# First weights on a second issuing queue, the norm vector inside the first x^T transfer, the last stores on two queues, and a gate product moved ahead

## The chip, the cores and the metric

The kernel runs on one core of a Trainium2 chip. The metric is the device time of one execution in microseconds (us). The kernel before takes 1500.37 us, the median of three runs (1499.43 to 1500.54).

## The reference

One layer of a streaming encoder on 256 tokens of width 2048, all in float32. Shapes are given as (rows x columns).

```python
u = rmsnorm(x, norm_mix)                                   # 256 x 2048
z = u @ w_in                                               # 2048 x 15360
p, q, k, v, g_ret, g_pool, g_rt = split(z)                 # 1024, 1024, 1024, 2048, 2048, 2048, 2048
y_pool = pool_branch(p, w_group, scale) @ w_pool_proj      # 1024 x 2048: trailing means, linear map
y_ret  = retention_branch(q, k, v, g_ret) @ w_ret_proj     # 2048 x 2048: 8 heads, GroupNorm, silu gate
merged = sigmoid(g_pool) * y_pool + sigmoid(g_rt) * y_ret
h = x + merged @ w_out                                     # 2048 x 2048
ug = rmsnorm(h, norm_ffn) @ w_up                           # 2048 x 11264: gate half, up half
gate = causal_conv3(ug[:, :5632], conv_w) + conv_b
h = h + (silu(gate) * ug[:, 5632:]) @ w_down               # 5632 x 2048
out = h * rsqrt(mean(h * h) + 1e-6) * norm_final
```

## The kernel before, in words

Every large product is done to nearly float32 accuracy with float32r matmuls: each operand is cut into a high part (`hi`, written by ScalarE, line 82) and the rest (`lo`, by VectorE, line 83), and `mm3` (lines 89 to 92) adds three matmuls, hi by hi, hi by lo and lo by hi. Weights come in blocks of 128 partitions x 2048 floats (1 MB) on SyncE's queue (line 97), three buffers deep. A block is four k-tiles of 128 x 512 (in `w_up` it is 16 of 128 x 128). Its two halves of 128 x 1024 are split one after the other into three pairs of `hi` and `lo` buffers.

`product` (lines 213 to 227) makes 512 output columns for both blocks of 128 tokens (`tb` 0 and 1): per k-tile six matmuls of 512 columns. Its two sums sit in one of two PSUM pairs (`acc_pair`, two buffers in turn), so that a product needs the pair of the product before last. After each four k-tiles `tick` runs one small step from the list `side` (transposes, retention, pooling).

The stages follow one another: the first product with `w_in` (lines 155 to 173, operands arriving in small pieces), the rest of `w_in` with rotary embedding, retention and pooling, the sigmoid gates, then lines 459 to 486, the merge, then `w_out`, `w_up` with the convolution, and `w_down`. A tile framework orders the instructions of each engine and places the semaphores; a DMA takes one of eight completion semaphores in turn, and waits until the DMA that had it before has landed.

The places that the change touches:

- The head, lines 133 to 173. VectorE clears `warm`, ten bf16 matmuls on it occupy TensorE, and SyncE issues the norm vector (`nmix`, 128 x 16, line 143), then by turns a piece of x^T (line 160, 256 columns per k-tile) and a piece of weights (line 162, 512 columns per k-tile): first one k-tile each, again one, and then two at a time. Line 86 (ScalarE) multiplies x^T by `nmix` and rounds it to the high part, line 87 (VectorE) makes the rest, and lines 82 and 83 do the weights.
- The merge. For each of four column blocks `nb`, a product with `w_pool_proj` (8 k-tiles, sums `psp`) is followed by one with `w_ret_proj` (16 k-tiles, `psr`). Behind both, VectorE multiplies `psp` by its sigmoid (line 471) and `psr` by its own (line 472) and adds (line 473), for `tb` 0 and then 1.
- The tail, lines 588 to 667. `residual` adds the last sums to `h` in two halves (line 594), squares them with a running sum (line 597, ScalarE) and multiplies by the final norm vector (line 600). `finish` makes 1/sqrt of the mean square (lines 605 to 613) and scales and stores four pieces of 128 x 512 (lines 619 to 622), by VectorE and ScalarE in turn, all stored by SyncE. `finish` for `tb` 0 runs beside the matmuls of `tb` 1; for `tb` 1 nothing runs beside it.

Of the kernel before, what the change touches and what calls it, by code (L numbers as in the profile page):

```python
# [16 lines left out]
P = 128  # L17
D = 2048
# [25 lines left out]
def tile_block(ctx: ExitStack, tc: tile.TileContext, ins, out):  # L44
# [85 lines left out]
            side.popleft()()  # L130


    warm = const.tile([P, NB], BF16, tag="warm", name="warm")
    dve.memset(warm, 0.0)
    warm_a = small.tile([P, 1], F32, tag="warm_a", name="warm_a", bufs=1)
# [3 lines left out]
        pe.matmul(warm_ps, warm[:, :P], warm, start=True, stop=True)  # L139


    nmix = const.tile([P, KT], F32, tag="nmix", name="nmix")
    sp.dma_start(nmix, ins["nmix"])
    uh = [unit(F32R) for _ in range(2)]
    ul = [unit(F32R) for _ in range(2)]

    def kview(pair, kt):
        return pair[kt // 8][:, (kt % 8) * T : (kt % 8 + 1) * T]

    NB_P, NB_Q, NB_K, NB_V, NB_GR, NB_SP, NB_SR = 0, 2, 4, 6, 10, 14, 18  # L150
    first = {}
    xt = [unit() for _ in range(2)]
    raws = {}
    done = 0
    for n in (1, 1) + (2,) * 7:
        g, at = divmod(done, 4)
        if at == 0:
            raws[g] = wraw.tile([P, 2048], F32, tag="raw", name=nm("raw"))
        x2 = xt[done // 8][:, (done % 8) * T : (done % 8 + n) * T]
        sp.dma_start(x2, ins["xt"][:, done * T : (done + n) * T])  # L160
        w2 = raws[g][:, at * NB : (at + n) * NB]
        sp.dma_start(w2, ins["w_in"][NB_Q * 4 + g][:, at * NB : (at + n) * NB])
        for j in range(n):
            k = done + j
            split_scaled(kview(uh, k), kview(ul, k), x2[:, j * T : (j + 1) * T], nmix[:, k : k + 1])
        if at % 2 == 0:
            hi = wsplit.tile([P, 1024], F32R, tag="hi", name=nm("hi"))
            lo = wsplit.tile([P, 1024], F32R, tag="lo", name=nm("lo"))
            first[g, at // 2] = (hi, lo)
        for j in range(n):  # L170
            o = slice((at + j) % 2 * NB, ((at + j) % 2 + 1) * NB)
            split(hi[:, o], lo[:, o], w2[:, j * NB : (j + 1) * NB])
        done += n


    trig = const.tile([P, 2 * TB * 64], F32, tag="trig", name="trig")
# [282 lines left out]
    for nb in range(4):  # L459
        psp = product(  # L460
            ins["w_pool_proj"],
            nb * 2,
            8,
            lambda k: mix_h[:, k * T : (k + 1) * T],
            lambda k: mix_l[:, k * T : (k + 1) * T],
        )
        psr = product(ins["w_ret_proj"], nb * 4, KT, lambda k: kview(ret_h, k), lambda k: kview(ret_l, k))
        for tb in range(TB):
            a, b = t2k(), t2k()
            s = slice(tb * 1024 + (nb % 2) * NB, tb * 1024 + (nb % 2 + 1) * NB)  # L470
            dve.tensor_tensor(a, psp[tb], sgp[nb // 2][:, s], ALU.mult)  # L471
            dve.tensor_tensor(b, psr[tb], sgr[nb // 2][:, s], ALU.mult)  # L472
            dve.tensor_tensor(a, a, b, ALU.add)

            def turn(a=a, nb=nb, tb=tb):
                pt = aux_tile()
                for c in range(4):
                    pe.transpose(pt[:, c * P : (c + 1) * P], a[:, c * P : (c + 1) * P], ident)  # L478
                n0 = (nb % 2) * 4
                dst = [  # L480
                    x[nb // 2].rearrange("p (k t) -> p k t", t=T)[:, n0 : n0 + 4, tb * P : (tb + 1) * P]
                    for x in (mg_h, mg_l)
                ]
                split(dst[0], dst[1], pt.rearrange("p (c t) -> p c t", t=P))

            side.append(turn)
# [101 lines left out]
    def residual(tb, nb, ps):  # L588

        n = NB // 2 if nb == 3 else NB  # L590
        g = t2k() if nb == 3 else h[tb][:, nb * NB : (nb + 1) * NB]
        for c in range(0, NB, n):
            s = slice(nb * NB + c, nb * NB + c + n)
            dve.tensor_tensor(h[tb][:, s], ps[:, c : c + n], h[tb][:, s], ALU.add)
            junk = t2k()
            i = nb + c // n
            act.activation(junk[:, :n], h[tb][:, s], AF.Square, accum_out=ssq3[:, tb, i : i + 1])
        for c in range(0, NB, n):
            s = slice(nb * NB + c, nb * NB + c + n)
            dve.tensor_tensor(g[:, c : c + n], h[tb][:, s], gf[:, s], ALU.mult)  # L600
        return g

    def finish(tb, last):
        a, v, y, q = (small.tile([P, 1], F32, tag=f"fin{i}", name=nm("fin")) for i in range(4))
        dve.tensor_scalar(a, ssq3[:, tb, 3:4], 1.0 / D, part[:, tb : tb + 1], ALU.mult, ALU.add)
        act.activation(y, ssq3[:, tb, 4:5], AF.Sqrt, scale=1.0 / D, bias=a)
        dve.tensor_scalar(v, ssq3[:, tb, 4:5], 1.0 / D, a, ALU.mult, ALU.add)

        r = small.tile([P, 1], F32, tag="fin_r", name=nm("r"))
        dve.reciprocal(y, y)  # L610
        dve.tensor_scalar(q, y, y, v, ALU.mult, ALU.mult)
        dve.tensor_scalar(q, q, -0.5, 1.5, ALU.mult, ALU.add)
        dve.tensor_tensor(r, y, q, ALU.mult)
        for nb in range(4):
            s = slice(nb * NB, (nb + 1) * NB)
            g = last if nb == 3 else h[tb][:, s]
            o = t2k()
            if nb % 2 == 0:
                dve.tensor_scalar(o, g, r, None, ALU.mult)
            else:  # L620
                act.activation(o, g, AF.Copy, scale=r)
            sp.dma_start(out[tb * P : (tb + 1) * P, s], o)

    for nb in range(3):
        ps = product(ins["w_down"], nb * 11, NFF, lambda k: kview(ah, k), lambda k: kview(al, k))
# [12 lines left out]
    for g in range(NFF // 4):  # L638
# [11 lines left out]
        for hf, (wh, wl) in enumerate(halves):  # L650
            for j in range(2):
# [9 lines left out]
                    mm(1)  # L661
                else:
                    held.append(mm)
    finish(0, residual(0, 3, ps[0]))
    for mm in held:
        mm(1)
    finish(1, residual(1, 3, ps[1]))

# [11 lines left out]
def _arrays(np, x, norm_mix, w_in, w_pool_group, pool_scale, w_pool_proj, ret_gn_gain,  # L682
            w_ret_proj, w_out, norm_ffn, w_up, conv_w, conv_b, w_down, norm_final):
    f = np.float32
    a = {}
    x = np.asarray(x)[0]
    a["xt"] = np.ascontiguousarray(x.T.reshape(KT, P, T).transpose(1, 0, 2)).reshape(P, KT * T)
    a["x"] = x.reshape(TB, P, D)
    a["w_in"] = _blocks(np.asarray(w_in)[0], np)
    a["w_pool_proj"] = _blocks(np.asarray(w_pool_proj)[0], np)  # L690
    a["w_ret_proj"] = _blocks(np.asarray(w_ret_proj)[0], np)
    a["w_out"] = _blocks(np.asarray(w_out)[0], np)
    a["w_down"] = _blocks(np.asarray(w_down)[0], np)
    up = np.asarray(w_up)[0].reshape(KT, P, 2, NFF, P).transpose(3, 2, 1, 0, 4)
    a["w_up"] = np.ascontiguousarray(up).reshape(2 * NFF, P, KT * P)
    g = np.asarray(w_pool_group)[0].reshape(4, 2, P, 256).transpose(2, 0, 1, 3)
    a["w_pool_group"] = np.ascontiguousarray(g).reshape(P, 2048)
    cw = np.asarray(conv_w)[0].reshape(3, NFF, P).transpose(2, 0, 1).reshape(P, 3 * NFF)
    a["vecs"] = np.concatenate(
        [  # L700
            _columns(np.asarray(norm_ffn)[0]),
            _columns(np.asarray(ret_gn_gain)[0]),
            _columns(np.asarray(pool_scale)[0]),
            cw,
            _columns(np.asarray(conv_b)[0]),
        ],
        axis=1,
    )
    a["nmix"] = np.ascontiguousarray(_columns(np.asarray(norm_mix)[0]))
    a["norm_final"] = np.asarray(norm_final).reshape(1, D)  # L710

    t = np.arange(T)
    inv = 10000.0 ** (-np.arange(64) / 64.0)
    ang = t[:, None].astype(f) * inv.astype(f)[None, :]
    ang = ang.astype(np.float64)
    trig = np.stack([np.cos(ang), np.sin(ang)], axis=1).astype(f)
    a["trig"] = np.ascontiguousarray(trig.reshape(TB, P, 128).transpose(1, 0, 2)).reshape(P, 2 * TB * 64)
    log_g = np.log(1.0 - 2.0 ** (-5.0 - np.arange(HEADS)))
    j, i = t[:, None], t[None, :]
    gap = np.where(j // CHUNK <= i // CHUNK, np.abs(i - j), np.inf)  # L720
# [30 lines left out]
```

## Time and profile before

| | |
|---|---|
| time, median of 3 | 1500.37 us |
| profiled execution | 1500.19 us, of which the span in the trace is 1498.4 us |
| granted TensorE clock | 0.998 of full speed |
| TensorE busy | 1480.2 us, 99% of the span |
| VectorE / ScalarE busy | 911.1 us (61%) / 698.2 us (47%) |
| DMA | 287.01 MB, mean 192 GB/s; 336 GB/s in the first fortieth of the span |

TensorE is busy at 9 tenths or more in each of the forty slices but the last. Busy time alone therefore says little about where time can be saved: the waits and the chain of work show it.

### The profile page before, as it was taken

The page shows a single profiled execution, that of the slowest core. Times are in us where ns is not written, and L with a number is a line of the kernel's source. Part 1 is how long each engine was busy: PE and PEld are TensorE (multiplying, and loading weights), DVE is VectorE, ACT ScalarE, POOL GpSimd, SP SyncE. Part 2 cuts the span into 40 slices and gives each one's busy share as a digit, 9 for nine tenths or more (in the row PEclk, how much of TensorE's full clock was granted, in tenths as well). Part 3 has the DMA queues.
Part 4 walks back from the last instruction along what each step waited for, and adds up shares of the span by engine and source line. Part 5 has one row for each costly group of instructions (what it writes and reads, how often), then busy time and mean ns, then how long its engine had stood idle before and what let it go on. Part 6 is the DMA issues. An engine that isn't in the chain of part 4 may idle for free.

```text
span 1498.4 us, 18277 instructions
## 1 busy us (share of the span) xinstructions
PE 1480.2 (99%) x7286; PEld 1243.5 (83%) x7286; DVE 911.1 (61%) x1229; ACT 698.2 (47%) x899; POOL 0.2 (0%) x4
## 2 busy tenths in 40 slices
PE   9999999999999999999999999999999999999997
PEld 6888888888888877778888888888888888888886
DVE  5765865675444455555577777777766766445454
ACT  6545444455444433334455444444454444344343
POOL 0000000000000000000000000000000000000000
PEclk9999999999999999999999999999999999999999
DMA  9654555464555555565545555555555555555553
GB/s 336 208 204 161 189 192 195 165 212 178 171 194 197 197 180 185 197 211 182 191 174 193 176 194 185 182 196 178 187 194 176 193 187 211 195 194 196 197 196 113
DMA packets 42710, 287.01 MB, mean 192 GB/s; under 512 B 4993, under 2 KB 5633, under 8 KB 9089
## 3 DMA queue, kind: packets, MB, share of 16 engines
q1 hardware_dynamic: 42624, 285.84, 54.9%
q8 instruction: 57, 0.93, 0.2%
q14 instruction: 29, 0.23, 0.0%
HBM read 283.73 MB, written 2.10 MB: 191 GB/s over the span
## 4 chain that ended last, share of the span: by engine, by line
PE 98%; DVE 1%; DMA 1%; SPq 0%; issue 0%; ACT 0%; ACTq 0%
PE acc L90 21%; PE acc L92 20%; PE acc L91 20%; PE acc L556 20%; PE acc L557 10%; PE acc L560 1%; PE aux L91 1%; PE aux L92 1%; PE aux L90 1%; PE acc L559 1%; DMA raw<-in_w_in 1%; PE aux L248 0%; PE aux L478 0%; PE aux L341 0%; DVE lo L83 0%; DVE t L472 0%
## 5 line engine op out<-in xcount | busy, mean ns | idle before, releaser
L83 DVE TENSOR_TENSOR lo<-raw,hi 128x1024 fp32r<-128x1024 f32 (+1 forms) x526 | 634.6, 1208 | 460.3 <-ACT hi L82 460.2
L82 ACT ACTIVATE hi<-raw 128x1024 fp32r<-128x1024 f32 (+1 forms) x526 | 549.3, 1046 | 588.6 <-PE acc L92 438.8
L90 PE MATMUL acc<-hi,u 128*128 128x512 f32 x1336 | 524.1, 392 | 5.9 <-DVE t L471 5.9
L92 PE MATMUL acc<-hi,u 128*128 128x512 f32 x1336 | 520.6, 390 | 0.0
L91 PE MATMUL acc<-lo,u 128*128 128x512 f32 x1336 | 520.0, 389 | 0.0
L556 PE MATMUL acc<-u,hi 128*128 128x512 f32 x1320 | 470.2, 399 | 0.0
L557 PE MATMUL acc<-u,lo 128*128 128x256 f32 x1320 | 370.8, 281 | 0.0
L90 PEld LDWEIGHTS acc<-hi,u 128*128 128x128 f32 x1336 | 250.9, 188 | 57.8 <-ACT hi L82 7.5
L556 PEld LDWEIGHTS acc<-u,hi 128*128 128x128 f32 x1320 | 248.0, 188 | 56.9
L92 PEld LDWEIGHTS acc<-hi,u 128*128 128x128 f32 x1336 | 250.7, 188 | 53.3
L91 PEld LDWEIGHTS acc<-lo,u 128*128 128x128 f32 x1336 | 251.1, 188 | 50.3
L557 PEld LDWEIGHTS acc<-u,lo 128*128 128x128 f32 x1320 | 249.3, 189 | 4.2
L565 ACT ACTIVATE t<-acc 128x256 f32<-128x256 f32 x88 | 29.1, 382 | 70.5 <-PE acc L560 70.5
L568 DVE TENSOR_TENSOR t<-acc,t 128x256 f32<-128x256 f32 x88 | 33.3, 420 | 45.5 <-ACT t L565 45.5
L82 ACT ACTIVATE u<-t 128x256 fp32r<-128x256 f32 x44 | 18.3, 417 | 51.6 <-DVE t L578 51.6
L560 PE MATMUL acc<-u,hi 128*128 128x512 f32 x88 | 35.2, 400 | 0.0
L570 DVE TENSOR_TENSOR t<-t,rb 128x512 f32<-128x512 f32 x44 | 30.5, 693 | 1.5
L83 DVE TENSOR_TENSOR u<-t,u 128x256 fp32r<-128x256 f32 x44 | 18.6, 424 | 19.3 <-ACT u L82 19.3
L86 ACT ACTIVATE u<-aux,vecs 128x256 fp32r<-128x256 f32 x40 | 18.7, 469 | 23.6 <-DVE u L87 22.7
L559 PE MATMUL acc<-u,lo 128*128 128x256 f32 x88 | 24.9, 283 | 0.0
L87 DVE SCALAR_TENSOR_TENSOR u<-aux,vecs,u 128x256 fp32r<-128x256 f32 x40 | 19.1, 481 | 8.7 <-ACT u L86 8.7
L271 ACT ACTIVATE u<-acc,y 128x512 f32<-128x512 f32 x24 | 15.2, 686 | 17.0 <-PE acc L92 17.0
(132 smaller groups left out, 538.9 us busy)
## 6 DMA issues: line engine op xcount, KB each, us to landing
raw<-in_w_up SPq DMA_DIRECT2D x88, 1024.0 KB, 4.9
raw<-in_w_in SPq DMA_DIRECT2D x84, 1024.0 KB, 4.9
raw<-in_w_down SPq DMA_DIRECT2D x44, 1024.0 KB, 4.9
raw<-in_w_ret_proj SPq DMA_DIRECT2D x16, 1024.0 KB, 4.9
raw<-in_w_out SPq DMA_DIRECT2D x16, 1024.0 KB, 4.9
raw<-in_w_pool_proj SPq DMA_DIRECT2D x8, 1024.0 KB, 5.0
u<-in_x SPq DMA_DIRECT2D x4, 1024.0 KB, 7.7
raw<-in_w_in SPq DMA_DIRECT2D x7, 512.0 KB, 8.5
```

The lines of the kernel that those rows point to most:

```text
L82: act.activation(hi, src, AF.Copy)
L83: dve.tensor_tensor(lo, src, plain(hi), ALU.subtract)
L90: pe.matmul(o, ah, bh, start=start, stop=False)
L91: pe.matmul(o, ah, bl, start=False, stop=False)
L92: pe.matmul(o, al, bh, start=False, stop=stop)
L556: pe.matmul(o[half], wh[:, s], both, start=kt == 0, stop=False)
L557: pe.matmul(o[half][:, :T], wl[:, s], both[:, :T], start=False, stop=False)
L559: pe.matmul(o[half][:, :T], wl[:, s], both[:, :T], start=False, stop=False)
L560: pe.matmul(o[half], wh[:, s], both, start=False, stop=True)
L565: act.activation(small_part[:, half * T : (half + 1) * T], o[half][:, T:], AF.Copy)
L568: dve.tensor_tensor(gu[:, h2], o[half][:, :T], small_part[:, h2], ALU.add)
L570: dve.tensor_tensor(gv, gv, rb.unsqueeze(1).broadcast_to([P, 2, T]), ALU.mult)
```

## The change

Four edits, which are independent in what they compute; the output is the same function of the inputs.

1. The head. The norm vector is put in front of x^T in device memory, so that one row of that input is 16 + 4096 floats, and the first transfer brings `nmix` and the first piece of x^T as one tile `front` of 128 x 272. The first three pairs of transfers are issued ahead of the clearing of `warm`, and the two weight pieces of one k-tile each go out on ScalarE's queue.
2. The merge. The two multiplications of `psp` by its sigmoid stand between the two products.
3. The tail's scalar chain. The first addend `a` is computed between the two halves of the multiplication by the final norm vector.
4. The stores. ScalarE scales the first quarter and stores it by its own queue; VectorE scales the other three, and SyncE stores them.

```diff
+    front = const.tile([P, KT + T], F32, tag="front", name="front")
+    nmix = front[:, :KT]
+    pieces = ((0, 1), (1, 1)) + tuple((k, 2) for k in range(2, KT, 2))
...
+    def load_x(k, n):
+        if k == 0:
+            return sp.dma_start(front, ins["xt"][:, : KT + T])
+        return sp.dma_start(x_piece(k, n), ins["xt"][:, KT + k * T : KT + (k + n) * T])
+
+    def load_w(k, n, eng):
+        return eng.dma_start(w_piece(k, n), ins["w_in"][NB_Q * 4 + k // 4][:, k % 4 * NB : (k % 4 + n) * NB])
+
+    for k, n in pieces[:3]:
+        tc.keep_in_program_order(load_x(k, n))
+        tc.keep_in_program_order(load_w(k, n, act if n == 1 else sp))
...
-    nmix = const.tile([P, KT], F32, tag="nmix", name="nmix")
-    sp.dma_start(nmix, ins["nmix"])
...
-        sp.dma_start(x2, ins["xt"][:, done * T : (done + n) * T])
...
-        sp.dma_start(w2, ins["w_in"][NB_Q * 4 + g][:, at * NB : (at + n) * NB])
+        if k0 > 2:
...
+            load_x(k0, n)
+            load_w(k0, n, sp)
...
+        cols = [slice(tb * 1024 + (nb % 2) * NB, tb * 1024 + (nb % 2 + 1) * NB) for tb in range(TB)]
+        gated = [t2k() for _ in range(TB)]
+        for tb in range(TB):
+            dve.tensor_tensor(gated[tb], psp[tb], sgp[nb // 2][:, cols[tb]], ALU.mult)
         psr = product(ins["w_ret_proj"], nb * 4, KT, lambda k: kview(ret_h, k), lambda k: kview(ret_l, k))
         for tb in range(TB):
-            a, b = t2k(), t2k()
-            s = slice(tb * 1024 + (nb % 2) * NB, tb * 1024 + (nb % 2 + 1) * NB)
-            dve.tensor_tensor(a, psp[tb], sgp[nb // 2][:, s], ALU.mult)
-            dve.tensor_tensor(b, psr[tb], sgr[nb // 2][:, s], ALU.mult)
+            a, b = gated[tb], t2k()
+            dve.tensor_tensor(b, psr[tb], sgr[nb // 2][:, cols[tb]], ALU.mult)
             dve.tensor_tensor(a, a, b, ALU.add)
...
+            if c:
+
+                a = small.tile([P, 1], F32, tag="fin0", name=nm("fin"))
+                dve.tensor_scalar(a, ssq3[:, tb, 3:4], 1.0 / D, part[:, tb : tb + 1], ALU.mult, ALU.add)
             dve.tensor_tensor(g[:, c : c + n], h[tb][:, s], gf[:, s], ALU.mult)
...
-        dve.tensor_scalar(a, ssq3[:, tb, 3:4], 1.0 / D, part[:, tb : tb + 1], ALU.mult, ALU.add)
...
-            if nb % 2 == 0:
+            if nb:
                 dve.tensor_scalar(o, g, r, None, ALU.mult)
             else:
                 act.activation(o, g, AF.Copy, scale=r)
-            sp.dma_start(out[tb * P : (tb + 1) * P, s], o)
+            (sp if nb else act).dma_start(out[tb * P : (tb + 1) * P, s], o)
...
-    a["xt"] = np.ascontiguousarray(x.T.reshape(KT, P, T).transpose(1, 0, 2)).reshape(P, KT * T)
+    xt = np.ascontiguousarray(x.T.reshape(KT, P, T).transpose(1, 0, 2)).reshape(P, KT * T)
+    a["xt"] = np.concatenate([_columns(np.asarray(norm_mix)[0]), xt], axis=1)
```

On VectorE, at the end of the first column block of the merge, this stands before. `acc_3949` holds the sums of the `w_pool_proj` product of this block, `acc_4018` those of its `w_ret_proj` product, and `acc_4165` those of the next block's `w_pool_proj` product, which takes the pair of `acc_3949`; lines 471, 472 and 473 are the two gates and the addition.

```order
L472 TENSOR_TENSOR t_4156<-acc_4018,u_2699 128x512
L471 TENSOR_TENSOR t_4160<-acc_3949,u_2697 128x512
L473 TENSOR_TENSOR t_4155<-t_4155,t_4156 128x512
L472 TENSOR_TENSOR t_4161<-acc_4018,u_2699 128x512
L83 TENSOR_TENSOR lo_4210<-raw_4207,hi_4209 128x1024
L473 TENSOR_TENSOR t_4160<-t_4160,t_4161 128x512
L83 TENSOR_TENSOR lo_4214<-raw_4207,hi_4213 128x1024
L83 TENSOR_TENSOR lo_4252<-raw_4249,hi_4251 128x1024
L83 TENSOR_TENSOR u_3947<-aux_4200,u_3945 128x4x128
L83 TENSOR_TENSOR lo_4256<-raw_4249,hi_4255 128x1024
L471 TENSOR_TENSOR t_4385<-acc_4165,u_2697 128x512
```

On VectorE, the same place after the change. `acc_4021` is now the `w_ret_proj` pair, `acc_4164` the next block's `w_pool_proj` pair; lines 489, 493 and 494 are the gates and the addition.

```order
L493 TENSOR_TENSOR t_4158<-acc_4021,u_2698 128x512
L493 TENSOR_TENSOR t_4161<-acc_4021,u_2698 128x512
L494 TENSOR_TENSOR t_4017<-t_4017,t_4158 128x512
L494 TENSOR_TENSOR t_4018<-t_4018,t_4161 128x512
L83 TENSOR_TENSOR lo_4209<-raw_4206,hi_4208 128x1024
L83 TENSOR_TENSOR lo_4213<-raw_4206,hi_4212 128x1024
L83 TENSOR_TENSOR lo_4255<-raw_4252,hi_4254 128x1024
L83 TENSOR_TENSOR u_3946<-aux_4199,u_3944 128x4x128
L83 TENSOR_TENSOR lo_4259<-raw_4252,hi_4258 128x1024
L489 TENSOR_TENSOR t_4247<-acc_4164,u_2696 128x512
L489 TENSOR_TENSOR t_4248<-acc_4164,u_2696 128x512
```

The gate of `tb` 1's `w_pool_proj` sums has left the group behind the `w_ret_proj` product and stands with that of `tb` 0 behind the `w_pool_proj` product; in front of the third `lo` half of the next block (`lo_4210`, now `lo_4209`) there are four instructions as before.

On SyncE's queue, at the program's start, this stands before; `u` is the buffer of x^T, `raw` that of the weights.

```order
L143 DMA nmix<-in_nmix 128x16
L160 DMA u_100<-in_xt 128x256
L162 DMA raw_102<-in_w_in 128x512
L160 DMA u_100<-in_xt 128x256
L162 DMA raw_102<-in_w_in 128x512
L160 DMA u_100<-in_xt 128x512
L162 DMA raw_102<-in_w_in 128x1024
L160 DMA u_100<-in_xt 128x512
L162 DMA raw_129<-in_w_in 128x1024
```

On SyncE's queue after the change, the same transfers up to the weights of k-tiles 4 and 5 (`raw_128`):

```order
L148 DMA front<-in_xt 128x272
L149 DMA u_80<-in_xt 128x256
L149 DMA u_80<-in_xt 128x512
L152 DMA raw_82<-in_w_in 128x1024
L149 DMA u_80<-in_xt 128x512
L152 DMA raw_128<-in_w_in 128x1024
```

Three issues have left SyncE's queue: `nmix` is gone, and the first two weight pieces stand on ScalarE's queue, ahead of its table load. The eight instructions in front of the weights of k-tiles 4 and 5 have become five.

On VectorE, at the end of the program (`tb` 1), before and then after the change; `ssq` holds the sums of squares, `u_9963` and `u_9962` the final norm vector.

```order
L594 TENSOR_TENSOR u_4861<-acc_11121,u_4861 128x256 x2
L600 TENSOR_TENSOR t_11527<-u_4861,u_9963 128x256 x2
L605 TENSOR_SCALAR fin_11536<-ssq_9965,part 128x1
L607 TENSOR_SCALAR fin_11537<-ssq_9965,fin_11536 128x1
L610 RECIPROCAL fin_11538<-fin_11538 128x1
```

```order
L616 TENSOR_TENSOR u_4860<-acc_11120,u_4860 128x256 x2
L626 TENSOR_TENSOR t_11526<-u_4860,u_9962 128x256
L625 TENSOR_SCALAR fin_11534<-ssq_9964,part 128x1
L626 TENSOR_TENSOR t_11526<-u_4860,u_9962 128x256
L632 TENSOR_SCALAR fin_11537<-ssq_9964,fin_11534 128x1
L635 RECIPROCAL fin_11538<-fin_11538 128x1
```

The addend of line 605 (now 625) has moved in front of the second half of the multiplication.

## Rows read from the trace of the kernel before

**Rows 1.** The page's chain of work that ended last, by engine.

```profile
PE 98%; DVE 1%; DMA 1%; SPq 0%; issue 0%; ACT 0%; ACTq 0%
```

**Rows 2.** Waits of TensorE: line, waited for, us in total, times, longest.

```profile
PE acc L90 <- DVE t L471: 5.9, 4, 1.5
```

**Rows 3.** Timeline, first merge boundary: start, us, engine, line, operation [idle before].

```profile
552.03 0.39 PE L92 MATMUL acc<-hi,u 128*128 128x512 f32 x1
...
552.45 0.69 DVE L472 TENSOR_TENSOR t<-acc,u 128x512 f32<-128x512 f32 x1 [0.40 <-PE acc L92]
553.06 0.68 DVE L471 TENSOR_TENSOR t<-acc,u 128x512 f32<-128x512 f32 x1
...
553.89 0.47 PE L90 MATMUL acc<-hi,u 128*128 128x512 f32 x1 [1.47 <-DVE t L471]
...
554.26 0.68 DVE L472 TENSOR_TENSOR t<-acc,u 128x512 f32<-128x512 f32 x1
...
554.86 1.22 DVE L83 TENSOR_TENSOR lo<-raw,hi 128x1024 fp32r<-128x1024 f32 x1
```

**Rows 4.** The chain in order of time: merge boundaries, products of w_out.

```profile
552.19 0.24 PE acc L92
...
587.56 0.24 PE acc L92
...
688.45 0.44 PE aux L511 x4
...
711.18 0.44 PE aux L511 x4
```

**Rows 5.** Timeline of SyncE's queue at the start, duration of each issue.

```profile
0.73 0.39 SPq L143 DMA_DIRECT2D nmix<-in_nmix  x1
1.17 0.42 SPq L160 DMA_DIRECT2D u<-in_xt  x1
...
4.48 0.56 SPq L162 DMA_DIRECT2D raw<-in_w_in  x1
```

**Rows 6.** Timeline of the start, the other engines.

```profile
3.55 0.51 ACT L86 ACTIVATE u<-u,nmix 128x256 fp32r<-128x256 f32 x1 [1.33 <-DMA u<-in_xt]
...
12.96 1.15 ACT L82 ACTIVATE hi<-raw 128x512 fp32r<-128x512 f32 x2 [0.41 <-DMA raw<-in_w_in]
...
13.62 1.29 DVE L83 TENSOR_TENSOR lo<-raw,hi 128x512 fp32r<-128x512 f32 x2 [0.56 <-ACT hi L82]
...
14.37 0.50 PE L91 MATMUL aux<-lo,u 128*128 128x512 f32 x1 [0.22 <-DVE lo L83]
```

**Rows 7.** Stretches of the start: busy PE, PEld, DVE, ACT, POOL; clock, DMA share, GB/s.

```profile
2.00:3.00 1.00, 1.00 (x4) 0.44 (x3) 0.00 (x0) 0.21 (x2) 0.00 (x0) 1.00 0.55 168
3.00:4.00 1.00, 1.00 (x4) 0.32 (x3) 0.00 (x0) 0.45 (x1) 0.00 (x0) 1.00 0.81 178
4.00:5.00 1.00, 1.00 (x4) 0.25 (x2) 0.48 (x1) 0.06 (x1) 0.00 (x0) 1.00 0.83 189
...
14.00:16.00 2.00, 1.78 (x8) 1.39 (x8) 2.00 (x5) 1.91 (x5) 0.00 (x0) 1.00 1.03 408
```

**Rows 8.** Timeline of the tail after the last matmul.

```profile
1490.42 0.75 DVE L600 TENSOR_TENSOR t<-u,u 128x256 f32<-128x256 f32 x2
1490.53 0.19 ACT L597 ACTIVATION_READ_ACCUMULATOR t<-u 128x1 f32 x1
...
1490.93 0.18 ACT L597 ACTIVATION_READ_ACCUMULATOR t<-u 128x1 f32 x1
1491.09 0.21 DVE L605 TENSOR_SCALAR fin<-ssq,part 128x1 f32<-128x1 f32 x1
1491.39 0.29 ACT L606 ACTIVATE fin<-ssq,fin 128x1 f32<-128x1 f32 x1 [0.28 <-DVE fin L605]
...
1492.61 0.88 DVE L619 TENSOR_SCALAR t<-u,r 128x512 f32<-128x512 f32 x2
```

**Rows 9.** A stretch of the last stores, columns as in Rows 7.

```profile
1494.00:1495.00 1.00, 0.00 (x0) 0.00 (x0) 0.00 (x0) 0.00 (x0) 0.00 (x0) 0.50 1.02 385
```

More of the change, by code (lines that the diff above doesn't have):

```diff
@@ L130, in flush, with x_piece, w_piece @@
             side.popleft()()
+    front = const.tile([P, KT + T], F32, tag="front", name="front")
+    nmix = front[:, :KT]
+    xt = [unit() for _ in range(2)]
+    NB_P, NB_Q, NB_K, NB_V, NB_GR, NB_SP, NB_SR = 0, 2, 4, 6, 10, 14, 18
+    raws = {0: wraw.tile([P, 2048], F32, tag="raw", name=nm("raw"))}
+    pieces = ((0, 1), (1, 1)) + tuple((k, 2) for k in range(2, KT, 2))
+    def x_piece(k, n):
+        return front[:, KT:] if k == 0 else xt[k // 8][:, (k % 8) * T : (k % 8 + n) * T]
+    def w_piece(k, n):
+        return raws[k // 4][:, k % 4 * NB : (k % 4 + n) * NB]
+    def load_x(k, n):
[7 more added lines that the diff above has]
+        tc.keep_in_program_order(load_w(k, n, act if n == 1 else sp))
     warm = const.tile([P, NB], BF16, tag="warm", name="warm")
@@ L148, in kview @@
         return pair[kt // 8][:, (kt % 8) * T : (kt % 8 + 1) * T]
-    NB_P, NB_Q, NB_K, NB_V, NB_GR, NB_SP, NB_SR = 0, 2, 4, 6, 10, 14, 18
     first = {}
[L152 to L159, printed above, removed]
-        sp.dma_start(x2, ins["xt"][:, done * T : (done + n) * T])
-        w2 = raws[g][:, at * NB : (at + n) * NB]
-        sp.dma_start(w2, ins["w_in"][NB_Q * 4 + g][:, at * NB : (at + n) * NB])
+    for k0, n in pieces:
+        g, at = divmod(k0, 4)
+        if k0 > 2:
+            if at == 0:
+                raws[g] = wraw.tile([P, 2048], F32, tag="raw", name=nm("raw"))
+            load_x(k0, n)
+            load_w(k0, n, sp)
+        x2, w2 = x_piece(k0, n), w_piece(k0, n)
         for j in range(n):
-            k = done + j
+            k = k0 + j
             split_scaled(kview(uh, k), kview(ul, k), x2[:, j * T : (j + 1) * T], nmix[:, k : k + 1])
@@ L172, in tile_block @@
             split(hi[:, o], lo[:, o], w2[:, j * NB : (j + 1) * NB])
-        done += n
     trig = const.tile([P, 2 * TB * 64], F32, tag="trig", name="trig")
@@ L591, in residual @@
         g = t2k() if nb == 3 else h[tb][:, nb * NB : (nb + 1) * NB]
+        a = None
         for c in range(0, NB, n):
@@ L599, in residual, with finish @@
             s = slice(nb * NB + c, nb * NB + c + n)
+            if c:
+                a = small.tile([P, 1], F32, tag="fin0", name=nm("fin"))
+                dve.tensor_scalar(a, ssq3[:, tb, 3:4], 1.0 / D, part[:, tb : tb + 1], ALU.mult, ALU.add)
             dve.tensor_tensor(g[:, c : c + n], h[tb][:, s], gf[:, s], ALU.mult)
-        return g
-    def finish(tb, last):
-        a, v, y, q = (small.tile([P, 1], F32, tag=f"fin{i}", name=nm("fin")) for i in range(4))
-        dve.tensor_scalar(a, ssq3[:, tb, 3:4], 1.0 / D, part[:, tb : tb + 1], ALU.mult, ALU.add)
+        return g, a
+    def finish(tb, last, a):
+        v, y, q = (small.tile([P, 1], F32, tag=f"fin{i}", name=nm("fin")) for i in range(1, 4))
         act.activation(y, ssq3[:, tb, 4:5], AF.Sqrt, scale=1.0 / D, bias=a)
@@ L663, in tile_block @@
                     held.append(mm)
-    finish(0, residual(0, 3, ps[0]))
+    finish(0, *residual(0, 3, ps[0]))
     for mm in held:
         mm(1)
-    finish(1, residual(1, 3, ps[1]))
+    finish(1, *residual(1, 3, ps[1]))
 def _blocks(w, np):
@@ L708, in _arrays @@
     )
-    a["nmix"] = np.ascontiguousarray(_columns(np.asarray(norm_mix)[0]))
     a["norm_final"] = np.asarray(norm_final).reshape(1, D)
```

## The prediction

> **What bounds the kernel now.** I read the chain of waits first: 98% of the time that decides the end lies on TensorE [rows 1]. A change can then gain only where TensorE stands still, and this one touches the three places where it does: the start, the four ends of a merge block, and the tail behind the last matmul. The view of waits gives the middle one: four waits of TensorE for line 471, 5.9 us in all, 1.5 the longest [rows 2]. The timeline shows what one is [rows 3]. The last matmul of a block begins at 552.03. Its sums come free for VectorE at 552.45, which does line 472 for `tb` 0 first and line 471 for `tb` 1 behind it, to about 553.7. Only that line frees the PSUM pair that the next block's first matmul writes, and it starts at 553.89. The pair's sums had been complete since the end of the `w_pool_proj` product, sixteen k-tiles earlier. VectorE was told to read them late.
>
> At the start the chain is a transfer: the weights of k-tiles 4 and 5 are issued at 4.48 [rows 5] and reach ScalarE at 12.96. Its split, and VectorE's, let the matmul at 14.37 go [rows 6]. That is the last wait of the first product.
>
> **The merge (part 2).** What a boundary costs is best taken from the chain. From one block's end to the next is 587.56 - 552.19 = 35.37 us [rows 4]. A product with `w_out` has the sixteen k-tiles and two sets of four transposes without such a wait: 711.18 - 688.45 = 22.73 us [rows 4]. Less two transposes at 0.44, that is 21.85 us for 96 matmuls, 0.228 each. The merge block has 48 matmuls more, so 22.73 + 10.92 = 33.65 without a wait, and 35.37 - 33.65 = 1.72 us are lost. The wait alone is 1.47 [rows 3]; the rest is restarting. The ends are 4 x 1.47 = 5.9 and 4 x 1.72 = 6.9. I take 6.9, since it counts whole periods.
>
> What is late next? VectorE still has four instructions behind a block's end, and behind them the third `lo` half of the next block, at 554.86 for 1.22 us, so ready at 556.1 [rows 3]. TensorE, no longer held, needs that half after 24 matmuls and four transposes: 552.03 + 0.23 + 5.47 + 0.44 = 558.2. That leaves 2.1 us. In the middle of the block line 489 now runs twice, 0.69 each, ahead of the third `lo` half of `w_ret_proj`: about 0.4 + 1.4 + 1.2 = 3.0 us behind the product's end, where the two halves already split last 5.5. The pair of `psr` is free 1.8 us into the next block, which needs it 11 us in. No new wait of TensorE follows, and the work added is none: the same twelve multiplications and additions, in another order.
>
> **The head (part 1).** Three issues leave SyncE's queue ahead of the deciding transfer. The first x^T piece takes the place of `nmix`, 1.17 - 0.73 = 0.44 us earlier, and the deciding issue is five issues of about 0.45 behind 0.73, at 3.0 instead of 4.48: 1.5 us earlier [rows 5]. But a transfer that is issued earlier lands earlier only where the DMA engines had room. Between 2 and 5 us they were busy 0.55, 0.81 and 0.83 of the time [rows 7]: 0.45 + 0.19 + 0.17 = 0.81 us of room, a part of it because the second and third transfers were not yet issued. The start itself moves by 0.44. So 0.44 is had from the earlier start alone, up to 1.25 with all the room filled. I take 0.8, between the two. ScalarE's two issues, 2 x 0.47 = 0.94 at SyncE's pace, lie in the 1.33 us in which it stood idle ahead of its first x^T piece [rows 6]. When that piece comes 0.44 earlier, 0.05 us of cover is lost, at a place where TensorE is not yet waited for. The bounds are wide, since the trace has no transfer on ScalarE's queue and no row of x^T that begins 64 bytes into a line. At best the DMA moves at the 408 GB/s of 14 to 16 us from the start [rows 7], which is a rival below. At worst the x^T of six k-tiles, 786 KB, goes at the 178 GB/s of 3 to 4 us instead of 408 [rows 7]: 4.4 us instead of 1.9, a loss of 2.5 less the 0.44, so 2.0.
>
> A rule of the Trainium skill speaks against this part (DMA: Bandwidth & Descriptors, "How a descriptor splits into AXI transactions"): a descriptor that doesn't start on a multiple of 256 bytes needs one read more, so a 2 KB row nine instead of eight. By that rule, an estimate from the page, x^T would take an eighth longer, 0.2 us on the way to the deciding transfer; the head would give 0.6 and the sum come to 7.7. No row of this trace shows it.
>
> **The tail (parts 3 and 4).** The addend (line 605) starts at 1491.09 behind both halves of line 600, although its sum of squares was read out at 1490.53 + 0.19 = 1490.72. The square root (line 606) waits for it until 1491.39 [rows 8]. Between the halves the addend can start at about 1490.42 + 0.38 = 1490.80 and is done at 1491.01. The root then waits for its other input, read out at 1490.93 + 0.18 = 1491.11, and starts near 1491.15: 0.24 earlier. VectorE's second half and the instruction behind it end some 0.1 later than the root, if nothing overlaps; so 0.12 to 0.24, and I take 0.2. For the stores, VectorE's first output, ready about 0.45 us behind 1492.61, goes to SyncE at once in both kernels, and from 1494 on the DMA engines are full, at 1.02 of their time and 385 GB/s [rows 9]. Four stores of 256 KB then take 2.7 us however they are issued. Cover: the engines are the bound, not the issuing queue; worth 0, with the tail's 0.2 from the earlier start alone. For `tb` 0 the same edits lie beside the matmuls of `tb` 1 and cost nothing.
>
> **Sum.** 6.9 + 0.8 + 0.2 = 7.9 us. The profiled execution took 1500.19, 1.8 more than its span: 1500.19 - 7.9 = 1492.3. The median of the runs is 0.18 above that execution. I forecast 1492.3.
>
> **Rivals.**
> - *The start runs at full rate.* With two queues filled at once the DMA moves 408 GB/s from 2 us on. The 2.36 MB up to k-tile 5 need 5.8 us, and TensorE is bound by its own 24 matmuls: it begins near 5 us, when the warming matmuls end [rows 7], and reaches k-tile 4 at about 10.6 instead of 14.4, 3.8 earlier: 1500.19 - 6.9 - 3.8 - 0.2 = 1489.3. For it: the low GB/s of 2 to 5 us. Against it: the engines were already busy 0.8 there. Chance 0.12.
> - *The head loses*, by the worst bound: 1500.19 - 6.9 + 2.0 - 0.2 = 1495.1. Chance 0.08.
> - *A wait takes the place of the one removed.* If VectorE comes 2.1 us later than counted at a boundary, TensorE stands before the third `lo` half and the merge gives nothing: 1500.19 - 0.8 - 0.2 = 1499.2. Against it: the order in front of that half is four instructions as before. Chance 0.06, half of that with part of the gain left.
> - *Slower: x^T comes too slowly to feed the first product.* Rows that start 64 bytes late are read f times slower. Two k-tiles need 262 KB of x^T (0.64 us at 408 GB/s) and 524 KB of weights (1.29), while TensorE takes 24 x 0.228 = 5.5 us for four, 2.7 for two. The first six k-tiles lose 1.9 x (f - 1), and each of the five later pairs 1.29 + 0.64 f - 2.7. From about f = 3.4 this eats the 7.9; at f = 4 it is 5.7 + 5 x 1.15 = 11.5, and the time 1503.8. Against it: between 2 and 5 us, at its slowest, the DMA was 408 / 168 = 2.4 times slower than later [rows 7]. Chance 0.03.
>
> **How the numbers follow.** The forecast has 0.71, the rivals 0.12, 0.08, 0.06 and 0.03. The range, 1490.0 to 1495.2, holds the forecast's own spread (head 0 to 1.5, merge 5.9 to 6.9: 1491.5 to 1494.3), a third of the first rival and the second: about 0.82. A measurement of this kernel can tell a change of about 0.2%, 3.0 us, from none. Faster than 1497.4: 0.71 + 0.12 + 0.08 + 0.03 of the third, 0.94. Within 3 us: 0.03. Slower: 0.03.
>
> **What would show it.** In the profile after, TensorE has no wait for a merge gate, and blocks follow one another every 33.6 to 33.7 us. The last wait of the first product ends near 13.6 instead of 14.37, the root starts 0.2 us sooner behind the last matmul, and the stores keep the DMA engines full as before. A wait of TensorE for a `lo` half 6 us into a merge block, or blocks over 34 us, would break the first term; a last head wait later than 14.4 the second.

## The result: 8.8 us faster, and the profile after

The changed kernel takes 1491.24 us, the median of four runs (1490.98 to 1491.49). The kernel before took 1500.07 beside it (1499.43 to 1500.54). The ratio is 0.9941, with a 95% interval of 0.9924 to 0.9959. The profiled execution takes 1491.38 us against 1500.19, so 8.81 less, where the sum had 7.9.

Three marks in the trace split this: the first transposes behind the first product, the last transposes inside the `w_out` product, and the last matmul. The lines are from the timeline of TensorE (start, us, engine, line, operation), of the kernel before:

```profile
74.10 0.60 PE L248 MATMUL aux<-ident,t 128*128 128x128 f32 x4
...
754.29 0.60 PE L511 MATMUL aux<-ident,u 128*128 128x128 f32 x4
...
1489.33 0.39 PE L92 MATMUL acc<-u,u 128*128 128x512 f32 x1
```

The same marks after:

```profile
72.39 0.60 PE L267 MATMUL aux<-ident,t 128*128 128x128 f32 x4
...
745.55 0.60 PE L532 MATMUL aux<-ident,u 128*128 128x128 f32 x4
...
1480.68 0.39 PE L92 MATMUL acc<-u,u 128*128 128x512 f32 x1
```

The first mark comes 1.71 us earlier, which is the head. From the first to the second it was 680.19 and is 673.16: 7.03 less, the merge. From the second to the third it is 735.04 and 735.13, so 0.09 more, in a stretch that the change doesn't touch. The span ends 9.09 behind the start of the last matmul before, and 8.91 after: the tail, 0.18. Together 8.83.

**The merge.** These are all the waits of TensorE in the kernel after (what, total, times, longest). The group of four for 5.9 us [rows 2] is gone, and nothing has come in its place:

```profile
PE aux L165 <- DVE warm L160: 1.2, 1, 1.2
PE aux L90 <- ACT hi L82: 0.4, 1, 0.4
PE aux L91 <- DVE lo L83: 0.2, 1, 0.2
PE aux L556 <- DVE dg L555: 0.2, 1, 0.2
```

The first boundary in the timelines of TensorE and VectorE, against [rows 3]:

```profile
550.32 0.39 PE L92 MATMUL acc<-hi,u 128*128 128x512 f32 x1
550.54 0.39 PE L90 MATMUL acc<-hi,u 128*128 128x512 f32 x1
...
550.74 1.29 DVE L493 TENSOR_TENSOR t<-acc,u 128x512 f32<-128x512 f32 x2 [0.40 <-PE acc L92]
551.95 1.28 DVE L494 TENSOR_TENSOR t<-t,t 128x512 f32<-128x512 f32 x2
553.15 1.22 DVE L83 TENSOR_TENSOR lo<-raw,hi 128x1024 fp32r<-128x1024 f32 x1
...
556.66 0.40 PE L91 MATMUL acc<-lo,u 128*128 128x512 f32 x1
```

The next block's first matmul starts 0.22 behind the last one; before the change it started 1.86 behind. VectorE still does its four instructions, now beside TensorE. The third `lo` half is ready at 553.15 + 1.22 = 554.37, and the matmul at 556.66 is its first reader: 2.3 us of slack. The chain shows the period, here by the first transposes of the first and of the fourth block's result, against [rows 4]:

```profile
556.15 0.44 PE aux L499 x4
...
656.99 0.44 PE aux L499 x4
```

Three periods lie between: (656.99 - 556.15) / 3 = 33.61 us each, instead of 35.37.

**The head.** Timeline of the start after, against [rows 5, 6]:

```profile
0.73 0.91 ACTq L152 DMA_DIRECT2D raw<-in_w_in  x2
0.73 0.38 SPq L148 DMA_DIRECT2D front<-in_xt  x1
...
3.21 0.74 SPq L152 DMA_DIRECT2D raw<-in_w_in  x1
...
4.95 0.51 ACT L86 ACTIVATE u<-front 128x256 fp32r<-128x256 f32 x1 [1.79 <-DMA front<-in_xt]
...
8.52 1.16 ACT L82 ACTIVATE hi<-raw 128x512 fp32r<-128x512 f32 x2 [0.37 <-DMA raw<-in_w_in]
...
9.93 0.50 PE L91 MATMUL aux<-lo,u 128*128 128x512 f32 x1 [0.22 <-DVE lo L83]
...
10.47 1.15 ACT L82 ACTIVATE hi<-raw 128x512 fp32r<-128x512 f32 x2
```

The weights of k-tiles 4 and 5, issued at 3.21 instead of 4.48, are split from 10.47 on, 2.49 us earlier than the 12.96 of [rows 6], and are waited for no longer: the row at 10.47 has no idle time in front of it. TensorE's last wait of the first product ends at 9.93, on the weights of k-tiles 2 and 3. Twelve matmuls, 2.73 us, lie between that matmul and the one of k-tile 4 where it used to wait until 14.37, so its end answers to 14.37 - 2.73 = 11.64, and 11.64 - 9.93 = 1.71 is the gain. On the other side, x^T's first piece reaches ScalarE at 4.95, later than the 3.55 of [rows 6].

The stretches of the start after (columns as in [rows 7]):

```profile
2.00:3.00 1.00, 1.00 (x4) 0.44 (x3) 0.00 (x0) 0.99 (x2) 0.00 (x0) 1.00 0.88 195
3.00:4.00 1.00, 1.00 (x4) 0.31 (x3) 0.00 (x0) 0.16 (x1) 0.00 (x0) 1.00 0.92 175
4.00:5.00 1.00, 1.00 (x4) 0.30 (x2) 0.00 (x0) 0.05 (x1) 0.00 (x0) 1.00 0.97 305
5.00:8.00 3.00, 2.60 (x9) 1.27 (x7) 2.30 (x5) 2.86 (x6) 0.00 (x0) 1.00 1.00 378
8.00:11.00 3.00, 2.78 (x12) 1.95 (x12) 2.58 (x6) 2.63 (x6) 0.00 (x0) 1.00 0.99 387
```

The last two of them before:

```profile
5.00:8.00 3.00, 1.76 (x7) 1.16 (x7) 1.69 (x3) 1.84 (x4) 0.00 (x0) 1.00 0.95 335
8.00:11.00 3.00, 2.54 (x10) 1.52 (x9) 1.91 (x4) 1.84 (x4) 0.00 (x0) 1.00 0.94 302
```

Between 2 and 5 us the DMA moved 140 KB more than before, 675 instead of 535; between 5 and 11 us 384 KB more, 3 x (43 + 85).

**The tail.** Timeline behind the last matmul after, against [rows 8]:

```profile
1482.50 0.29 ACT L631 ACTIVATE fin<-ssq,fin 128x1 f32<-128x1 f32 x1
...
1483.72 0.72 ACT L646 ACTIVATE t<-u,r 128x512 f32<-128x512 f32 x1 [0.92 <-DVE r L638]
...
1484.48 0.35 ACTq L647 DMA_DIRECT2D out<-t  x1
```

The root starts 1.82 us behind the last matmul's start, and started 2.06 behind it before (1491.39 - 1489.33): 0.24 earlier. The stores' stretch, against [rows 9]:

```profile
1485.00:1488.00 3.00, 0.00 (x0) 0.00 (x0) 0.00 (x1) 0.00 (x0) 0.00 (x0) 0.50 0.97 349
```

The DMA engines are nearly full again, and from the start of the output's first scaling to the last landing it is 4.98 us in both kernels. The second queue gave nothing there.

### The profile page after: what moved, and what is told of

Same layout as the page of the kernel before. It is cut to its first block, busy times and chain, and to the rows that moved or that the text cites. A ratio compares the mean times of both kernels' runs of the same rounds, so it can differ in the third digit from the quotient of the medians.

```text
span 1489.6 us, 18270 instructions
## 1 busy us (share of the span) xinstructions
PE 1479.1 (99%) x7286; PEld 1243.9 (84%) x7286; DVE 911.1 (61%) x1231; ACT 696.7 (47%) x897; POOL 0.2 (0%) x4
## 3 DMA queue, kind: packets, MB, share of 16 engines
q10 hardware_dynamic: 576, 1.05, 0.2%
## 4 chain that ended last, share of the span: by engine, by line
PE 98%; DVE 1%; DMA 0%; ACT 0%; issue 0%; SPq 0%; DVEq 0%
PE acc L90 21%; PE acc L92 21%; PE acc L91 20%; PE acc L577 20%; PE acc L578 10%; PE acc L581 1%; PE aux L91 1%; PE aux L92 1%; PE aux L90 1%; PE acc L580 1%; DMA raw<-in_w_in 0%; PE aux L499 0%; PE aux L360 0%; PE aux L267 0%; DVE lo L83 0%; PE aux L532 0%
```

## The experiments

The mark of the head below is the start of the first transposes behind the first product: 74.10 before, 72.39 after. It is read from one profile of each kernel. Four profiles with the head as after put it at 72.28 to 72.50, three with the head as before at 73.59 to 74.10. So two single marks that differ by half a microsecond lie hardly further apart than that scatter.

### The merge alone

The kernel before with the second edit of the change:

```diff
+            dve.tensor_tensor(gated[tb], psp[tb], sgp[nb // 2][:, cols[tb]], ALU.mult)
         psr = product(ins["w_ret_proj"], nb * 4, KT, lambda k: kview(ret_h, k), lambda k: kview(ret_l, k))
...
-            dve.tensor_tensor(a, psp[tb], sgp[nb // 2][:, s], ALU.mult)
```

> The kernel before with the merge edit alone. Theory: it carries four waits of 1.72 to 1.76 us, so 6.9 to 7.0 us less than before; blocks follow every 33.6 us and no wait of TensorE for a gate is left; head and tail as before (last wait of the first product ending near 14.4 us, unless the head's transfers differ from one execution to the next). Rival: the three edits help one another, and alone the merge gives under 6 us because another wait shows (a lo half of the next block).

Measured: 1492.80 us (1492.72 to 1492.96), ratio 0.9951 (0.9938 to 0.9965). TensorE has no wait for a merge gate, and from the first mark to the second it is 673.17 us, 7.02 less. The merge gives its size alone. The rest of the 7.4 fits the head of this execution, whose mark lies at 73.59 with the head unchanged.

### The head alone

The kernel before with the first edit, of which the core is:

```diff
+    for k, n in pieces[:3]:
+        tc.keep_in_program_order(load_x(k, n))
+        tc.keep_in_program_order(load_w(k, n, act if n == 1 else sp))
...
-    sp.dma_start(nmix, ins["nmix"])
```

> The kernel before with the head edit alone. Theory: 1.7 us less than before, as between the two profiles, with the last wait of the first product ending near 9.9 us on k-tile 2 and none behind it. Rival: the 1.7 us were one execution's luck with the transfers; then the last wait ends on k-tile 4 again, later than 13 us, and the time is 0.4 to 1.2 us less than before.

Measured: 1498.45 us (eleven runs, 1498.16 to 1498.58), ratio 0.9987 (0.9979 to 0.9996); the mark is at 72.28. The head is worth 1.7 us by both, twice what was forecast. The merge's waits stand as before, in the view of waits:

```profile
PE acc L90 <- DVE t L490: 5.9, 4, 1.5
```

### The tail alone

The kernel before with the third and fourth edits:

```diff
+            if c:
+                a = small.tile([P, 1], F32, tag="fin0", name=nm("fin"))
+                dve.tensor_scalar(a, ssq3[:, tb, 3:4], 1.0 / D, part[:, tb : tb + 1], ALU.mult, ALU.add)
...
-            sp.dma_start(out[tb * P : (tb + 1) * P, s], o)
+            (sp if nb else act).dma_start(out[tb * P : (tb + 1) * P, s], o)
```

> The kernel before with the two tail edits alone (addend between the halves, first quarter stored from ScalarE's queue). Theory: the root 0.24 us sooner behind the last matmul, the stores as long as before, 0.2 us less in all, which lies within the spread of the runs. Rival: the second queue overlaps the stores, and the end comes 0.5 us or more sooner.

Measured: 1499.93 us (eleven runs, 1498.95 to 1501.76), ratio 0.9999 (0.999 to 1.0008). The time alone can't show 0.2 us. The profile does: the root is 1.82 us behind the last matmul instead of 2.06, and the end 8.87 instead of 9.09.

### All first transfers on SyncE's queue

```diff
-        tc.keep_in_program_order(load_w(k, n, act if n == 1 else sp))
+        tc.keep_in_program_order(load_w(k, n, sp))
```

> The changed kernel with all first transfers on SyncE's queue (norm vector still inside the first x^T transfer). Theory: the second queue fills the room that issuing left between 2 and 5 us, and only with it do the weights of k-tiles 4 and 5 land before TensorE wants them; without it the last wait of the first product ends on k-tile 4 near 13.5 us and the time is about 1 us more than the changed kernel's, 7.7 us less than before. Rival: the missing norm vector transfer and its 128 small rows are what helped; then it is as fast as the changed kernel, 8.8 us less than before.

Measured: 1492.01 us (1491.47 to 1492.63), ratio 0.9947 (0.9933 to 0.996); the mark is at 72.93. Of the head's 1.71 the second queue makes 0.54 by the mark (0.77 by the medians), and the folded norm vector with the earlier issue the other 1.17; both are rough, since its five runs lie 1.2 us apart. In the timeline the weights of k-tiles 4 and 5 come at 11.77, between the 10.47 of the changed kernel and the 12.96 before. The view of waits has only two waits of 0.2 each, on the single weight pieces of the first two k-tiles. The starts of the matmuls show that the last hold is still on k-tile 4, as the theory had it: its second matmul starts 0.47 behind its first, at 13.18, where 0.23 is usual.

```profile
11.77 1.15 ACT L82 ACTIVATE hi<-raw 128x512 fp32r<-128x512 f32 x2 [0.40 <-DMA raw<-in_w_in]
...
12.71 0.39 PE L90 MATMUL aux<-hi,u 128*128 128x512 f32 x1
13.18 0.50 PE L91 MATMUL aux<-lo,u 128*128 128x512 f32 x1
```

### Two other shares of the second queue

All three first weight pieces on ScalarE's queue:

```diff
-        tc.keep_in_program_order(load_w(k, n, act if n == 1 else sp))
+        tc.keep_in_program_order(load_w(k, n, act))
```

> The changed kernel with the third weight piece (k-tiles 2 and 3) on ScalarE's queue too, so that SyncE's queue brings x^T alone up to k-tile 3. Theory: the engines are full in either case; the deciding weights of k-tiles 2 and 3 are issued 0.4 us sooner, and the gauge is 72.0 to 72.4, at most 0.4 us gained. Rival: the queues' interleaving decides; x^T gets half of the engines, its early pieces land 0.5 us sooner and the first product starts sooner, gauge under 72.0.

Only the first:

```diff
-        tc.keep_in_program_order(load_w(k, n, act if n == 1 else sp))
+        tc.keep_in_program_order(load_w(k, n, act if k == 0 else sp))
```

> The changed kernel with only the first weight piece on ScalarE's queue. Theory: between the changed kernel and the one with a single queue: gauge 72.4 to 72.9. Rival: less interleaving brings the first x^T piece and the first weights sooner than 4.9 and 5.2 us, and the gauge is under 72.2.

Measured: 1492.11 us both (1491.85 to 1492.51 and 1491.48 to 1492.45), ratios 0.9946 (0.9931 to 0.9961) and 0.9945 (0.993 to 0.996); the marks are at 73.65 and 73.06. Neither is better than two pieces, and both marks are later than forecast (72.0 to 72.4 and 72.4 to 72.9). With one piece, the weights of k-tiles 4 and 5 reach ScalarE at 11.89, and TensorE waits on k-tile 4 again. With three, the second and third pieces of x^T are late, and ScalarE waits 0.93 for each; its timeline shows the second of these waits:

```profile
8.46 0.91 ACT L86 ACTIVATE u<-u,front 128x256 fp32r<-128x256 f32 x2 [0.93 <-DMA u<-in_xt]
```

### The norm vector apart, both queues kept

```diff
+    tc.keep_in_program_order(sp.dma_start(nmix, ins["nmix"]))
...
-            return sp.dma_start(front, ins["xt"][:, : KT + T])
+            return sp.dma_start(front, ins["xt"][:, :T])
```

> The changed kernel with the norm vector in a transfer of its own again, first on SyncE's queue (x^T rows then begin where they did before), the first two weight pieces still on ScalarE's queue. The gauge is the start of the first transposes behind the first product: 74.1 us before, 72.4 changed, 72.9 with one queue. Theory: the vector's own issue pushes every later x^T piece back by 0.44 us and costs about 0.5 of the 1.7 us, so 72.9. Rival: the second queue alone carries the gain, and the gauge stays at 72.4; or the vector's small rows hold the engines up, and it is 73.5 or later.

Measured: 1492.75 us (1491.76 to 1493.07), ratio 0.9951 (0.9936 to 0.9966); the mark is at 73.90. This is 1.5 slower than the changed kernel, but the profile has something else in it than a late transfer. TensorE's timeline, and below it the stretches, both of this kernel:

```profile
6.59 0.73 PE L90 MATMUL aux<-hi,u 128*128 128x512 f32 x2 [1.70 <-ACT hi L82]
...
8.27 0.63 PE L91 MATMUL aux<-lo,u 128*128 128x512 f32 x1
8.70 0.63 PE L92 MATMUL aux<-hi,u 128*128 128x512 f32 x1
```

```profile
7.00:8.00 1.00, 1.00 (x4) 0.59 (x3) 1.00 (x3) 1.00 (x3) 0.00 (x0) 0.71 0.92 307
8.00:9.00 1.00, 1.00 (x4) 0.81 (x3) 1.00 (x4) 1.00 (x3) 0.00 (x0) 0.50 0.99 279
```

After a pause of 1.70 us the granted clock fell to 0.50, which is 1.2 GHz, and the matmuls followed each other every 0.43 us instead of 0.23 until 10.83. Three of the four runs took 1492.74 us or more; the fourth took 1491.76, so the fall may not come in every execution. That run has no profile.

### The same with thirteen warming matmuls

```diff
-WARM = 10
+WARM = 13
```

> The kernel with the norm vector's transfer apart, and thirteen warming matmuls instead of ten. With ten, its TensorE stood idle from 4.9 to 6.6 us, and the granted clock fell to 0.5 from about 7.3 to 10.6 us. Theory: its gauge of 73.9 (first transposes) is the clock's doing, not the transfers'; with TensorE busy to about 6.2 us the clock stays at 1.00 and the gauge comes to 72.4 to 72.8. Rival: the vector's transfer delays the data by itself, and the gauge stays later than 73.3 at full clock.

Measured: 1491.58 us (1491.46 to 1491.8), ratio 0.9942 (0.9925 to 0.9958); the mark is at 72.93. The granted clock is 1.00 in every stretch from 6 to 13 us, although TensorE's warming ends near 5.5, not 6.2, and it pauses here too. Its timeline, and below it a row of SyncE's queue:

```profile
7.02 0.49 PE L90 MATMUL aux<-hi,u 128*128 128x512 f32 x1 [1.55 <-ACT hi L82]
...
8.55 0.40 PE L91 MATMUL aux<-lo,u 128*128 128x512 f32 x1
8.78 0.39 PE L92 MATMUL aux<-hi,u 128*128 128x512 f32 x1
```

```profile
5.18 0.33 SPq L152 DMA_DIRECT2D raw<-in_w_in  x1
```

So of the 1.51 us by which the mark lay behind the changed kernel's, 0.97 were the clock's (1.2 by the medians) and 0.54 the separate transfer's (0.34 by the medians).

The trace shows where the separate transfer costs. The first product starts at 7.02 instead of 6.03, because x^T's first piece, issued 0.44 later, reaches ScalarE at 5.94 instead of 4.95. A second effect is hidden behind this one. With the norm vector in front, the weights of k-tiles 4 and 5 are the ninth transfer, and there are eight completion semaphores. So SyncE issues them only at 5.18, just after the first weights have landed at 5.16; in the changed kernel they are the eighth and go out at 3.21. TensorE doesn't wait for them here.

### Five warming matmuls in the changed kernel

```diff
-WARM = 10
+WARM = 5
```

> The changed kernel with five warming matmuls instead of ten. Theory: TensorE then stands idle from about 3.1 us to the first product near 6 us, the granted clock falls to 0.5 for some us in the first product, and the gauge (first transposes) comes 1 to 2 us later than 72.4. Rival: the idle stretch alone doesn't lower the clock, and the gauge stays at 72.2 to 72.6.

Measured: one run, 1491.89 us; the mark is at 73.03. TensorE stands idle for 2.4 us, until 5.93, and its matmuls start 0.43 apart until 9.51, which is the lower level. A stretch and the timeline:

```profile
7.00:8.00 1.00, 1.00 (x4) 0.81 (x3) 0.97 (x3) 1.00 (x3) 0.00 (x0) 1.00 1.02 358
```

```profile
8.23 0.63 PE L92 MATMUL aux<-hi,u 128*128 128x512 f32 x1
8.66 0.63 PE L90 MATMUL aux<-hi,u 128*128 128x512 f32 x1
```

The loss is 0.64 by the mark, where 1 to 2 had been forecast. That is less than eight matmuls at 0.2 us more each, since a slower TensorE waits less for the weights: the wait of 9.93 is not there. The column of the granted clock shows 1.00 in this stretch all the same: in these runs it printed the lower level only where the clock had risen before. The distance of the starts is what tells.

### x^T on multiples of 256 bytes

Rows of the input begin with 64 floats ahead of x^T, the norm vector and zeros, instead of 16 (`XO = 64`):

```diff
-        return sp.dma_start(x_piece(k, n), ins["xt"][:, KT + k * T : KT + (k + n) * T])
+        return sp.dma_start(x_piece(k, n), ins["xt"][:, XO + k * T : XO + (k + n) * T])
```

> The changed kernel with 64 floats instead of 16 in front of each x^T row (48 of them zero and not used), so that every x^T piece begins on a multiple of 256 bytes. By the Trainium skill's rule on descriptors (DMA: Bandwidth & Descriptors, How a descriptor splits into AXI transactions) the unaligned pieces cost an eighth of x^T's time, and the gauge (first transposes) comes about 0.2 us sooner than 72.4. Theory of the rows: no change beyond 0.3 us, since the DMA engines moved 400 GB/s with unaligned rows from 11 us on.

Measured: 1491.87 us (1491.74 to 1492.35), ratio 0.9946 (0.9929 to 0.9962); the mark is at 73.44. Alignment gained nothing; this kernel is 0.6 slower than the changed one (the profile, with the mark 1.05 later, is of the slowest of its four runs). The rule of the Trainium skill that the prediction weighed (DMA: Bandwidth & Descriptors, "How a descriptor splits into AXI transactions") would have made it some 0.2 faster, by the estimate that each read takes equally long. The time alone can't refute that, since something else made the kernel slower. The stretch from 11 to 14 us can, where the DMA engines are full in both kernels; first this kernel, then the changed one (columns as in [rows 7]):

```profile
11.00:14.00 3.00, 3.00 (x13) 2.53 (x14) 3.00 (x7) 2.90 (x7) 0.00 (x0) 1.00 1.03 408
```

```profile
11.00:14.00 3.00, 3.00 (x15) 2.49 (x14) 3.00 (x7) 2.92 (x8) 0.00 (x0) 1.00 1.03 408
```

An eighth more time for x^T, a third of the bytes, would be some 17 GB/s of 408. No such price shows. Why the kernel is later stays open; the first transfer carries 25 KB of zeros more (48 floats x 128 rows), under 0.1 us at 387 GB/s, and its piece reaches ScalarE at 5.73 instead of 4.95.

### Both gates behind the second product

```diff
+        psr = product(ins["w_ret_proj"], nb * 4, KT, lambda k: kview(ret_h, k), lambda k: kview(ret_l, k))
...
         for tb in range(TB):
             dve.tensor_tensor(gated[tb], psp[tb], sgp[nb // 2][:, cols[tb]], ALU.mult)
-        psr = product(ins["w_ret_proj"], nb * 4, KT, lambda k: kview(ret_h, k), lambda k: kview(ret_l, k))
```

The two multiplications are a loop of their own as in the change, but written behind the `w_ret_proj` product.

> The changed kernel with the two gates of the pool product written behind the retention product again, but as a group ahead of the other gates. Theory: what made TensorE wait was the order in which the gates were written, tb 0's second gate ahead of tb 1's first; the framework moves both first gates up by itself, as it did with tb 0's, and the merge blocks follow every 33.6 us as in the changed kernel. Rival: only the place between the products frees the pair early; then TensorE waits at each block's end, for 1.5 us or for half of it.

Measured: one run, 1491.44 us. The waits of TensorE have no merge gate, and VectorE's order of the merge is that of the changed kernel. The framework puts both gates at the earlier place by itself. What cost the kernel before 7 us was not the place between the products, but that the gate of `tb` 1 was written behind `psr`'s gate of `tb` 0, and so stayed behind the product that this one needs.

### More work for VectorE behind each block

```diff
+            for _ in range(3):
+                dve.tensor_tensor(b, a, b, ALU.add)
```

Six additions of 128 x 512 per block, whose results nobody uses.

> The changed kernel with six additional VectorE additions of 128x512 (three per tb, results unused) behind each merge block, some 3.7 us of VectorE work. Theory of the 2.1 us of slack: VectorE's third lo half then comes about 1.6 us too late, TensorE waits there at each of four boundaries, and the kernel is 5 to 7 us slower than the changed one. Rival: the slack is larger than counted (VectorE is busy 61% of the time), and the time stays within 1 us.

Measured: one run, 1494.57 us; from the first mark to the second it is 3.27 us more, 0.82 a block. The waits of TensorE and the first boundary's timelines:

```profile
PE acc L91 <- DVE lo L83: 1.5, 4, 0.8
```

```profile
553.12 3.69 DVE L496 TENSOR_TENSOR t<-t,t 128x512 f32<-128x512 f32 x6
...
556.63 0.60 PE L501 MATMUL aux<-ident,t 128*128 128x128 f32 x4
556.74 1.22 DVE L83 TENSOR_TENSOR lo<-raw,hi 128x1024 fp32r<-128x1024 f32 x1
...
558.01 0.50 PE L91 MATMUL acc<-lo,u 128*128 128x512 f32 x1 [0.24 <-DVE lo L83]
```

The third `lo` half is ready at 557.96 instead of 554.37, 3.6 us later. With 2.3 us of slack, 1.3 should reach TensorE. It loses 0.8, since the second set of transposes, 0.44, moves forward into the gap; that is why the kernel is 3.3 us slower, and not 5 to 7 as forecast. So the wait that was a rival in the prediction exists, at the place and at nearly the slack counted there; the change stays clear of it.

## Why the prediction was right, and where its size was off

The forecast was 1492.3 us and the median is 1491.24, 1.1 less. Nearly all of the difference is the head.

- **Merge, 6.9 forecast, 7.03 measured.** The step held: the wait went, no other came, and the whole period was the right measure, not the wait's own 5.9. The period without a wait was put at 33.65 and is 33.61; four times that difference is the 0.1. The slack was counted at 2.1 and is 2.3.
- **Head, 0.8 forecast, 1.71 measured.** That the weights of k-tiles 4 and 5 would land earlier was right; the term was mis-sized. The step that failed is the one that allowed an earlier issue only the DMA's room between 2 and 5 us, at most 1.25 us in all. The experiments give each part of the edit its share, by one profile each: one queue alone has 1.17, the second adds 0.54. In the stretches, more than two thirds of the extra bytes up to 11 us move after 5 us, where the prediction had counted no room at all, at 335 and then 302 GB/s before and 378 and 387 after. The busy share there rose only from 0.95 and 0.94 to 1.00 and 0.99, so it did not show the room that there was. The deciding transfer came 2.49 earlier. Only 1.27 of that is its earlier issue (3.21 instead of 4.48); the rest is a shorter way from issue to use, 7.26 instead of 8.48, for which the prediction had no term. The gain is less than that only because k-tiles 2 and 3 became the bound.
- **"The last wait ends near 13.6"** was wrong: it ends at 9.93, on another pair of k-tiles. The prediction followed one transfer and did not ask which would be the last wait if that one came much earlier.
- **"The start itself moves by 0.44"** failed in its reading: x^T's first piece came 1.4 us later, not 0.44 earlier. The second queue makes it late: with one queue the piece comes at 3.32. Against the kernel before nothing was lost by it: the first product starts at 6.03, where it started at 6.25 before, since the first weights came earlier.
- **Tail, 0.2 forecast, 0.18 measured**, with the root 0.24 sooner and the stores unchanged, as worked out. The second queue at the end was worth nothing here, where the DMA engines are nearly full.
- **The rivals.** The start at full rate went less than halfway to its 3.8: the DMA was busy 0.88 to 0.97 of the time from 2 to 5 us, but at 175 GB/s in one of these stretches. The losing head, the new wait and the slow x^T did not come.

What stays open: why the same busy share of the DMA moves 175 GB/s at 3 us and 387 at 8, and what of the 1.17 belongs to the norm vector and what to issuing ahead of the clearing. The norm vector's own 0.54 was measured with both queues only, in one profile.

## What to carry to other kernels

Where TensorE is the bound, take a stall at a boundary from whole periods, and look for a reader that was written behind something it does not need: its place among its neighbours costs, not the work. For the head, work out the landing of every early transfer, not of the last one waited for, since the wait goes to whichever comes next. Before a variant of a start is blamed on its transfers, compare the distance of the matmul starts: a pause may have cost the clock as well.

## What the runs showed of the hardware that was not expected

- Small differences at the start decided the level of TensorE's clock. With the norm vector apart, its warming matmuls started 0.22 apart, the upper level, from 4.08 to the end of the warming; then it paused 1.70 us, and ran at 1.2 GHz from about 7.4 to 10.8 us. With three warming matmuls more, a pause of 1.55 us left it at 2.4 GHz. The changed kernel, which pauses 0.40, shows no fall.
- The second issuing queue made the first transfer later and the deciding one earlier than the same transfers on one queue: x^T's first piece reaches ScalarE at 4.95 instead of 3.32, the weights of k-tiles 4 and 5 at 10.47 instead of 11.77.
